# Half of a projection's contraction by Strassen's products, the other half with the attention heads

## The chip, the cores and the metric

The kernel runs on one core of a Trainium2 chip. The metric is the device time of one execution in microseconds (us), lower is better. Engines: TensorE (PE) multiplies matrices and has a weight load (PEld) beside it; VectorE (DVE), ScalarE (ACT) and GpSimd (POOL) work element by element; SyncE (SP) issues the transfers (DMA). Each engine takes its instructions in a fixed order.

## The reference

One layer of an encoder with two kinds of attention heads. In short (`rms` divides by the root mean square and multiplies by a gain):

```python
u = rms(h, norm_w) @ w_in                         # (tokens, 2048) @ (2048, 6656)
qa, ka, va, za, qb, kb, vb, zb = split(u)         # 8 heads A (2 groups of k, v), 8 heads B, 128 wide
qa, ka = rope(rms(qa, q_norm_a)), rope(rms(ka, k_norm_a))
ya = softmax(qa @ ka.T / sqrt(128)) @ va * silu(za)          # every token to every token
qb, kb = rms(qb, q_norm_b), rms(kb, k_norm_b)
yb = (softmax over a window of 8 x 16 tokens, with a bias, and 16 meta tokens)(qb, kb, vb) * silu(zb)
out = h + concat(ya, yb) @ w_out                  # (tokens, 2048) @ (2048, 2048)
```

It is done for two sequences, a prompt of 1024 tokens and a sample of 256, each with the same 16 meta tokens ahead: 16 + 256 + 1024 = 1296 different tokens. All is float32.

## The kernel before

A full float32 product is made of three passes: both factors are split into a high part and a rest (`split`: ScalarE copies the high part, VectorE subtracts), and TensorE adds high x high, high x rest and rest x high. Features stand on the partitions. A strip is 128 of the 6656 columns of `w_in` (52 strips), and its contraction is 16 tiles of 128.

The tokens come in two chunks: `chunk1` has the meta tokens, the sample and 384 prompt tokens (656 in all), `chunk2` the other 640. `strips` runs a strip: for each of the 16 contraction tiles, three matmuls for each of two blocks of tokens (256 or 272, and 384; lines L128 to L130). `get_x` loads a tile of x when a strip first wants it, splits it unnormalised, and sums its squares; the tokens' scale is only known after the last tile, and is multiplied in when a strip's sums leave PSUM (`rb`, `eb`).

`chunk1` does the sample's attention and keeps its tokens' q, k, v and z in DRAM. `chunk2` then has for each head A four blocks of 256 prompt queries (`attend`; 52 matmuls each), between them `FILL_A` strips of the last `NL` heads B, so that TensorE has other work while VectorE and ScalarE make the softmax; then the first heads B with their windows (`attend_strip`). The blocks of the last `NL` heads B, the late blocks, are put between the column strips of the output projection (`outproj`): its first sixteen strips take only the mixed heads 0 to 7 and keep their sums (`pd`); at strip `LSTR` the heads 8 to 15 (`yh`) are loaded, and sixteen more strips finish. A block of attention has one chain: scores, the maximum over the keys (VectorE, then a reduction over the partitions on POOL), the subtraction, the exponential on ScalarE, the sum (again reduced on POOL), its reciprocal (`put_y`), the result `yt`, split and written to `yd`.

A scheduler sets the order in which each engine meets these pieces, from the order of the code, priorities (weights come 300 steps early) and the pools' buffers.

Of the kernel before, what the change touches and what calls it, by code (L numbers as in the profile page):

```python
# [12 lines left out]
F32 = mybir.dt.float32  # L13
F32R = mybir.dt.float32r
AF = mybir.ActivationFunctionType
ALU = mybir.AluOpType
# [3 lines left out]

P = 128
DM = 2048
KT = 16
NMETA = 16
# [3 lines left out]
C1P = 384  # L28
T1 = NMETA + NS + C1P
T2 = NP - C1P  # L30
# [7 lines left out]
NL = 4  # L38
FILL_A = 2
FILL_B = 1  # L40
LSTR = 12
YORD = (0, 4, 1, 5, 2, 6, 3, 7)
WCH = 4
OBL = [(0, 512), (512, 512), (1024, 256)]
QA, KA, VA, ZA, QB_, KB, VB, ZB = 0, 8, 10, 12, 20, 28, 36, 44


class Kern:
# [8 lines left out]
    def rsqrt(self, ms, n):  # L57

        nc = self.nc
        l = self.ev.tile([P, n], F32, tag="ev", name="rs_l")  # L60
        nc.scalar.activation(l[:], ms, AF.Ln)  # L61
        r0 = self.ev.tile([P, n], F32, tag="ev", name="rs_r0")
        nc.scalar.activation(r0[:], l[:], AF.Exp, scale=-0.5)
        nc.scalar.activation(l[:], r0[:], AF.Square, scale=0.5 ** 0.5)
        nc.vector.tensor_tensor(out=l[:], in0=ms, in1=l[:], op=ALU.mult)
        nc.vector.scalar_tensor_tensor(out=r0[:], in0=l[:], scalar=1.5, in1=r0[:], op0=ALU.subtract, op1=ALU.mult)
        return r0

    def start_chunk(self, src, T):

        self.xsrc, self.T, self.xs = src, T, {}
        self.acc = self.xr.tile([P, T], F32, tag="xr", name="xacc")
        self.rb = self.one.tile([P, T], F32, tag="rb", name="rb")
        self.eb = self.one.tile([P, T], F32, tag="eb", name="eb")

    def get_x(self, kt):
        nc = self.nc
        if kt not in self.xs:
            T, acc = self.T, self.acc
            r = self.xr.tile([P, T], F32, tag="xr", name="xr")  # L80
            self.lastx = nc.sync.dma_start(r[:], self.xsrc[:, kt, :]).ins
            h = self.x.tile([P, T], F32R, tag="xh", name="xh")
            l = self.x.tile([P, T], F32R, tag="xl", name="xl")
            w = self.nw[:, kt:kt + 1]
            nc.scalar.activation(h[:], r[:], AF.Copy, scale=w)  # L85
            nc.vector.scalar_tensor_tensor(out=l[:], in0=r[:], scalar=w, in1=h[:].bitcast(F32), op0=ALU.mult, op1=ALU.subtract)  # L86
            if kt == 0:
                nc.scalar.activation(acc[:], r[:], AF.Square, scale=DM ** -0.5)
            else:
                nc.scalar.activation(r[:], r[:], AF.Square, scale=DM ** -0.5)  # L90
                nc.vector.tensor_tensor(out=acc[:], in0=acc[:], in1=r[:], op=ALU.add)
            self.xs[kt] = (h[:], l[:])
            if kt == KT - 1:
                with self.tc.issue_after(self.lastx):
                    for d, c in self.consts:
                        nc.sync.dma_start(d[:], c)
                if self.xsrc is self.io["x1"]:
                    nc.scalar.mul(self.nqkw[:], self.qkw[:], -1.0)
                nc.gpsimd.partition_all_reduce(self.eb[:], acc[:], P, RED.add)
                nc.vector.tensor_scalar(out=self.eb[:], in0=self.eb[:], scalar1=EPS, scalar2=None, op0=ALU.add)  # L100
                for o in range(0, T, 328):
                    n = min(328, T - o)
                    rr = self.rsqrt(self.eb[:, o:o + n], n)
                    nc.scalar.mul(self.rb[:, o:o + n], rr[:], -1.0)
                nc.vector.tensor_scalar(out=self.eb[:], in0=self.eb[:], scalar1=EPS, scalar2=None, op0=ALU.mult)
        return self.xs[kt]

    def strips(self, jobs, getx):

        nc, tc = self.nc, self.tc  # L110
        out = [[pool.tile([P, 512], F32, tag=tag, name="pp") for pool, tag in pools] for _, _, pools in jobs]
        for c in range(KT // WCH):
            ws = []
            for src, _, _ in jobs:
                with tc.high_priority(offset=self.woff):
                    w = self.raw.tile([P, WCH, P], F32, tag="raw", name="wr")
                    self.lastw = nc.sync.dma_start(w[:], src[:, c * WCH:(c + 1) * WCH, :]).ins
                    wh = self.w.tile([P, WCH, P], F32R, tag="wh", name="wh")
                    wl = self.w.tile([P, WCH, P], F32R, tag="wl", name="wl")
                    self.split(wh[:], wl[:], w[:])  # L120
                    ws.append((wh, wl))
            for k in range(WCH):
                kt = c * WCH + k
                xh, xl = getx(kt)
                for (wh, wl), ps, (_, blocks, _) in zip(ws, out, jobs):
                    for p, (o, n) in zip(ps, blocks):
                        first, last = kt == 0, kt == KT - 1
                        nc.tensor.matmul(p[:, :n], wh[:, k, :], xh[:, o:o + n], start=first, stop=False)  # L128
# [773 lines left out]
```

## Time and profile before

| | |
|---|---|
| median of three runs | 2295.93 us (2295.69 to 2296.95) |
| the profiled execution | 2295.91 us, span 2294.1 us |
| TensorE busy | 2268.6 us, 99% |
| VectorE busy | 1601.9 us, 70% |
| ScalarE busy | 1104.6 us, 48% |
| POOL busy | 530.9 us, 23% |
| DMA, mean | 126 GB/s, 39.5% of the engines' time |

The span runs from the first to the last instruction; the time has 1.8 us more. Busy time is what the recorded instructions take; where matmuls are pipelined, their starts tell more than their durations, since these overlap. An instruction's row ends with the idle time of its engine ahead of it and with what ended it, where there was any.

### The profile page before, as it was taken

Reading aid. Unit: us, or ns where it says so; the run is one execution under the profiler, and the core shown is the slowest. Engines: PE = TensorE matmul, PEld = TensorE weight load, DVE = VectorE, ACT = ScalarE, POOL = GpSimd, SP = SyncE. Lnnn points to the kernel's source line nnn. Section 1 sums busy time; section 2 is a strip of 40 time slices with the busy share of each in tenths; the row PEclk is TensorE's granted clock in tenths of the full one; section 3 lists DMA queues with packets and bytes.
Section 4 is the critical chain, followed back from the end, with each engine's and each line's share of the span. In section 5 each row is a group of like instructions: output and inputs, shape, how many; then the busy total and the mean of one; then the engine's idle time right before and its main releaser. Section 6 shows DMA issues by size and latency. Waiting matters only on the chain.

```text
span 2294.1 us, 40464 instructions
## 1 busy us (share of the span) xinstructions
PE 2268.6 (99%) x15166; PEld 2192.9 (96%) x15166; DVE 1601.9 (70%) x3092; ACT 1104.6 (48%) x2400; POOL 530.9 (23%) x275
## 2 busy tenths in 40 slices
PE   7999999999999999999999999999999999999999
PEld 7999999999999999999999999999999888888888
DVE  6876775555555689999998989998777666652221
ACT  6654554444444566676666665665454333320000
POOL 0322232211121124223223314223233222210000
PEclk9999999999999999999999999999999999999999
DMA  6433333333333442222222222224444966657342
GB/s 199 137 111 112 110 105 111 107 106 106 102 108 107 134 153 72 90 86 75 91 93 87 88 81 75 87 84 138 116 133 115 336 214 191 191 182 277 133 136 79
DMA packets 205733, 290.17 MB, mean 126 GB/s; under 512 B 55360, under 2 KB 125408, under 8 KB 203488
## 3 DMA queue, kind: packets, MB, share of 16 engines
q1 hardware_dynamic: 205536, 287.58, 39.5%
q8 instruction: 119, 1.95, 0.4%
q14 instruction: 78, 0.64, 0.1%
HBM read 216.30 MB, written 64.63 MB: 122 GB/s over the span
## 4 chain that ended last, share of the span: by engine, by line
PE 54%; DVE 3%; ACT 1%; POOL 1%; issue 1%; DMA 1%; SPq 0%; DVEq 0%; POOLq 0%
PE pp L130 8%; PE pp L129 8%; PE pp L128 8%; PE pp L754 7%; PE pp L755 7%; PE pp L756 7%; PE po L393 2%; PE po L296 1%; PE po L294 1%; PE po L295 1%; PE sp L254 1%; PE sp L255 1%; PE sp L256 1%; POOL m L138 1%; PE sp L361 1%
## 5 line engine op out<-in xcount | busy, mean ns | idle before, releaser
L128 PE MATMUL pp<-xh,wh 128*128 128x384 f32 (+2 forms) x3328 | 1025.2, 311 | 11.8 <-ACT xh L85 11.6
L129 PE MATMUL pp<-xl,wh 128*128 128x384 f32 (+2 forms) x3328 | 1030.7, 310 | 1.1 <-DVE xl L86 0.8
L130 PE MATMUL pp<-xh,wl 128*128 128x384 f32 (+2 forms) x3328 | 1029.8, 311 | 0.0
L128 PEld LDWEIGHTS pp<-xh,wh 128*128 128x128 f32 x3328 | 624.1, 188 | 13.7 <-ACT xh L85 13.1
L129 PEld LDWEIGHTS pp<-xl,wh 128*128 128x128 f32 x3328 | 625.8, 188 | 3.4 <-DVE xl L86 3.3
L130 PEld LDWEIGHTS pp<-xh,wl 128*128 128x128 f32 x3328 | 625.7, 188 | 0.2
L55 DVE TENSOR_TENSOR wl<-wr,wh 128x512 fp32r<-128x512 f32 x480 | 368.7, 771 | 226.1 <-ACT wh L54 220.8
L54 ACT CAST wh<-wr 128x512 fp32r<-128x512 f32 x480 | 294.7, 617 | 416.2 <-PE pp L129 198.3
L138 POOL PARTITION_ALL_REDUCE m<-ms x104 | 246.4, 2369 | 423.2 <-ACT ms L136 299.9
L754 PE MATMUL pp<-yh,wh 128*128 128x512 f32 (+1 forms) x768 | 274.6, 358 | 2.5 <-DMA yh<-yd 2.5
L755 PE MATMUL pp<-yh,wh 128*128 128x512 f32 (+1 forms) x768 | 275.0, 358 | 0.0
L219 POOL PARTITION_ALL_REDUCE tot<-a x80 | 170.3, 2128 | 450.6 <-DVE a L217 450.5
L756 PE MATMUL pp<-yh,wl 128*128 128x512 f32 (+1 forms) x768 | 274.2, 358 | 0.0
L202 POOL PARTITION_ALL_REDUCE ma<-m x80 | 106.9, 1336 | 583.9 <-DVE m L200 570.2
L754 PEld LDWEIGHTS pp<-yh,wh 128*128 128x128 f32 x768 | 145.7, 190 | 24.0 <-DMA yh<-yd 2.6
L755 PEld LDWEIGHTS pp<-yh,wh 128*128 128x128 f32 x768 | 145.7, 190 | 20.9
L756 PEld LDWEIGHTS pp<-yh,wl 128*128 128x128 f32 x768 | 145.5, 190 | 20.8
L785 DVE TENSOR_TENSOR o<-pp,o 128x512 f32<-128x512 f32 (+1 forms) x48 | 28.5, 602 | 140.3 <-PE pp L756 140.3
L258 ACT COPY S<-sp 128x512 f32<-128x512 f32 x136 | 77.7, 581 | 61.1 <-PE sp L256 37.1
L275 ACT ACTIVATE S<-S 128x512 f32<-128x512 f32 x136 | 84.4, 629 | 30.1 <-DVE S L274 30.0
L61 ACT ACTIVATE rs_l<-m 128x384 f32<-128x384 f32 (+2 forms) x104 | 49.1, 472 | 102.4 <-DVE m L139 102.2
L55 DVE TENSOR_TENSOR pl<-S,ph 128x512 fp32r<-128x512 f32 x136 | 96.0, 719 | 0.0
(186 smaller groups left out, 3235.6 us busy)
## 6 DMA issues: line engine op xcount, KB each, us to landing
wr<-in_w_in SPq DMA_DIRECT2D x416, 256.0 KB, 3.2
yd<-yt SPq DMA_DIRECT2D x160, 128.0 KB, 2.4
yh<-yd SPq DMA_DIRECT2D x16, 1280.0 KB, 17.4
wr<-in_w_out SPq DMA_DIRECT2D x64, 256.0 KB, 4.0
pd<-o SPq DMA_DIRECT2D x16, 640.0 KB, 4.3
o<-pd SPq DMA_DIRECT2D x16, 640.0 KB, 5.0
bt<-in_bt SPq DMA_DIRECT2D x16, 576.0 KB, 5.3
vw<-vn SPq DMA_DIRECT2D x32, 256.0 KB, 3.6
```

The lines of the kernel that those rows point to most:

```text
L54: nc.scalar.copy(hi, full)
L55: nc.vector.tensor_tensor(out=lo, in0=full, in1=hi.bitcast(F32), op=ALU.subtract)
L128: nc.tensor.matmul(p[:, :n], wh[:, k, :], xh[:, o:o + n], start=first, stop=False)
L129: nc.tensor.matmul(p[:, :n], wh[:, k, :], xl[:, o:o + n], start=False, stop=False)
L130: nc.tensor.matmul(p[:, :n], wl[:, k, :], xh[:, o:o + n], start=False, stop=last)
L138: nc.gpsimd.partition_all_reduce(m2[:], ms[:], P, RED.add)
L202: nc.gpsimd.partition_all_reduce(ma[:], m1[:], P, RED.max)
L219: nc.gpsimd.partition_all_reduce(tot[:], a1[:], P, RED.add)
L275: nc.scalar.activation(s, s, AF.Exp, scale=SCALE)
L754: nc.tensor.matmul(p[:, :n], wh, yh[:, o:o + n], start=i == 0, stop=False)
L755: nc.tensor.matmul(p[:, :n], wh, yl[:, o:o + n], start=False, stop=False)
L756: nc.tensor.matmul(p[:, :n], wl, yh[:, o:o + n], start=False, stop=i == 7)
```

## The change

The contraction of the first projection is cut in two. `first_half` takes the contraction tiles 0 to 7 for all 1296 tokens and all 52 strips. Two strips, two halves of the tokens and two quarters of the contraction make a 2 x 2 by 2 x 2 product, and `strassen` does it with seven products in place of eight (the variant with few sums); each product is four tiles x two blocks of 320 or 328 columns x three passes. `operands` loads all of x, normalises it and builds the seven sets of token operands once; `mixed` builds the weights' for each pair of strips. The 26 pairs' sums go to DRAM (`ud`). Between the pairs, `ahead` splits x's tiles 8 to 15 and the weights of 32 strips for later, and keeps them in DRAM (`xd`, `wd`).

`second_half` loads the split x, and runs every strip's remaining eight tiles for all tokens at once (`project`; blocks of 272 or 256, 512 and 512), adds the kept sum (`add_kept`) and goes on as before. With no chunks, a head has five blocks (`run`: four of the prompt and one of the sample). The late heads are six in place of four, with five blocks each, spread over the first 13 column strips of the output projection; `FILL_B` is gone.

```diff
-NL = 4
-FILL_A = 2
-FILL_B = 1
-LSTR = 12
+NL = 6
+FILL_A = 3
+LSTR = 13
...
+ORDER = (1, 2, 5, 6, 3, 7, 4)
...
+    def mm(self, ps, w, x, k, o, first, last):
+        for b in range(2):
+            p = ps[:, b, o:HB]
+            wh, wl = w[:, 0, k, :], w[:, 1, k, :]
+            xh, xl = x[:, 0, b, o:], x[:, 1, b, o:]
+            self.nc.tensor.matmul(p, wh, xh, start=first, stop=False)
+            self.nc.tensor.matmul(p, wh, xl, start=False, stop=False)
+            self.nc.tensor.matmul(p, wl, xh, start=False, stop=last)
+    def product(self, w, x, o):
+        ps = self.bank()
+        for k in range(WCH):
+            self.mm(ps, w, x[k], k, o, k == 0, k == WCH - 1)
+        return ps
...
+    def token_scale(self, half):
+        nc = self.nc
+        acc = self.rb[half]
+        (m, r), (l, _) = self.stage("b22", 2 * half), self.stage("b22", 2 * half + 1)
+        nc.gpsimd.partition_all_reduce(m, acc[:], P, RED.add)
+        self.rsqrt(m, r, l)
+        nc.scalar.mul(acc[:], r, -1.0)
...
+        raw = [[self.stage(n, k) for n in ("t2", "t3")] for k in range(WCH)]
+        for half in range(2):
+            for kt in range(KT):
+                r, sq = self.stage("t4", kt % WCH)
+                if kt < KH:
+                    r = raw[kt % WCH][half][kt // WCH]
+                nc.sync.dma_start(r, io[f"x{half + 1}"][:, kt].rearrange("p (b c) -> p b c", b=2))
+                acc = self.rb[half][:]
+                nc.scalar.activation(sq if kt else acc, r, AF.Square, scale=DM ** -0.5)
+                if kt:
+                    nc.vector.tensor_tensor(out=acc, in0=acc, in1=sq, op=ALU.add)
+            self.token_scale(half)
+        self.B = B = {n: [None] * WCH for n in self.bm}
...
+        for c, n in enumerate(("b11", "b21")):
+            for k in range(WCH):
+                put(n, k, norm(0, c, k))
+        for k in range(WCH):
+            t1 = raw[k][0][0]
+            minus(t1, norm(1, 0, k), t1)
+            put("t1", k, t1)
+        for k in range(WCH):
+            t2, t4 = self.stage("b22", k)
+            minus(t2, norm(1, 1, k), raw[k][0][0])
+            minus(t4, raw[k][0][1], t2)
+            put("t2", k, t2)
+            put("t4", k, t4)
+        for k in range(WCH):
+            b22 = raw[k][1][1]
+            put("b22", k, b22)
+            t3 = self.ct("t3")[:]
+            minus(t3, b22, raw[k][1][0])
+            put("t3", k, t3)
...
+        mix(s1, a21, a22, ALU.add)
+        mix(s2, s1, a11, ALU.subtract)
+        mix(a21, a11, a21, ALU.subtract)
+        mix(s4, a12, s2, ALU.subtract)
+        return {1: a11, 5: s1, 6: s2, 3: s4, 7: a21, 2: a12, 4: a22}
...
+        def p2():
+            ps, c = self.product(w[2], B["b21"], o), self.ct("c11")
+            add(c, ps, t["u"], o)
+            self.keep_sum(2 * i, 0, c)
+        def p3():
+            ps, c = self.product(w[3], B["b22"], HM), self.ct("c12")
+            add(c, t["u"], t["p5"], HM)
+            add(c, ps, c, HM)
+            self.keep_sum(2 * i, 1, c)
...
+    def first_half(self):
+        tc = self.tc
+        w = [{}, {}]
+        more = [self.ps.tile([P, 2, WCH, P], F32, tag="ps", name="wr") for _ in range(2)]
+        full = [self.mixed(0, [self.wraw(self.raw, "raw") for _ in range(4)]), self.mixed(1, [t[:, j] for t in more for j in range(2)])]
+        self.operands()
+        steps = [self.strassen(i, w[i]) for i in range(2)]
+        for n in ORDER:
+            for i in range(2):
+                w[i][n] = self.wsplit(full[i][n])
+                steps[i][n]()
+        ahead = self.ahead()
+        units = 4 * KH + 2 * len(AHEAD)
+        n, done = NW // 2 - 2, 0
+        for i in range(n):
+            with tc.high_priority(offset=self.woff):
+                full = self.mixed(2 + i, [self.wraw(self.raw, "raw") for _ in range(4)])
+                w = {k: self.wsplit(full[k]) for k in ORDER}
+            step = self.strassen(2 + i, w)
+            for k in ORDER:
+                step[k]()
+            while done * (n - 1) < units * (i + 1) and next(ahead, self) is not self:
+                done += 1
...
+    def tile_products(self, ps, ws, kt, o, n):
+        wh, wl = (ws[kt // WCH][:, i, kt % WCH, :] for i in range(2))
+        xh, xl = (self.xs[kt][:, i, o:o + n] for i in range(2))
+        first, last = kt == 0, kt == KH - 1
+        self.nc.tensor.matmul(ps[:, :n], wh, xh, start=first, stop=False)
+        self.nc.tensor.matmul(ps[:, :n], wh, xl, start=False, stop=False)
+        self.nc.tensor.matmul(ps[:, :n], wl, xh, start=False, stop=last)
+    def add_kept(self, ps, u, n):
+        self.nc.vector.tensor_tensor(out=u[:], in0=ps[:, :n], in1=u[:], op=ALU.add)
+        return u
+    def project(self, s, blocks, evac, result=None):
+        ws, us = self.weights(s), self.kept(s, blocks)
+        for j, ((o, n), u) in enumerate(zip(blocks, us)):
+            ps = self.pp.tile([P, 512], F32, tag="pp", name="pp")
+            for kt in range(KH):
+                self.tile_products(ps, ws, kt, o, n)
+            evac(j, self.add_kept(ps, u, n), o, n)
+        return result
...
+    def run(self, h, *a):
+        for b in range(5):
+            self.run_block(h, b, *a)
+    def late_blocks(self):
+        for h in range(NH - NL, NH):
+            k, v = self.k_load(h), self.v_windows(h)
+            tab, q, z = self.bias_table(h), self.q_load(h), self.z_load(h)
+            for b in range(5):
+                self.run_block(NH + h, b, q, z, k, v, tab)
+                yield
...
-        done = 0
+        late, blocks, done = self.late_blocks(), 5 * NL, 0
         for c in range(16):
-            while done < 4 * NL and done * LSTR < 4 * NL * (c + 1):
-                next(self.late_blocks)
+            while done < blocks and done * LSTR < blocks * (c + 1):
+                next(late)
                 done += 1
```

Three places in the engines' orders. The first is VectorE at the start; `xl` is the rest of a tile of x, `xacc` and `rb` the sum of squares, `stage` a raw or built tile, `b_493` the first split operand. Before:

```order
L55 TENSOR_TENSOR wl<-wr,wh 128x512
L86 SCALAR_TENSOR_TENSOR xl<-xr,nw,xh 128x656
L55 TENSOR_TENSOR wl<-wr,wh 128x512 x3
L86 SCALAR_TENSOR_TENSOR xl<-xr,nw,xh 128x656 x2
L91 TENSOR_TENSOR xacc<-xacc,xr 128x656
```

and now, behind five splits and six mixes of weights and the first sum:

```order
L158 TENSOR_TENSOR rb<-rb,stage 128x656 x24
L78 SCALAR_TENSOR_TENSOR stage<-stage 128x656
L158 TENSOR_TENSOR rb<-rb,stage 128x656
L79 SCALAR_TENSOR_TENSOR stage<-stage 128x656
L158 TENSOR_TENSOR rb<-rb,stage 128x656 x2
L164 SCALAR_TENSOR_TENSOR stage<-stage,nw,rb 128x656 x6
L158 TENSOR_TENSOR rb<-rb,stage 128x656
L164 SCALAR_TENSOR_TENSOR stage<-stage,nw,rb 128x656 x2
L66 TENSOR_TENSOR b_493<-stage,b_493 128x656
```

The first split of x was the second thing on VectorE, and now stands behind sums, scale and multiplications; L78 and L79 are the scale of the first half of the tokens.

The second is TensorE in the prompt's attention; `sp` are scores, `po` values, `pp` a strip's sums. Before:

```order
L254 MATMUL sp<-q,kf 128x256
L255 MATMUL sp<-q,kf 128x256
L256 MATMUL sp<-q,kf 128x256
L128 MATMUL pp<-xh,wh 128x256
L129 MATMUL pp<-xl,wh 128x256
L130 MATMUL pp<-xh,wl 128x256
L128 MATMUL pp<-xh,wh 128x384
L129 MATMUL pp<-xl,wh 128x384
L190 MATMUL sm_ps<-q,km 48x256
```

and now, the end of one of the runs (58 matmuls from the last `pp` to the next):

```order
L519 MATMUL po<-ph,va 128x256
L520 MATMUL po<-ph,va 128x256
L521 MATMUL po<-pl,va 128x256
L522 MATMUL po<-Pm,vm_7131 128x256
L479 MATMUL sp<-q,kf 128x256
L480 MATMUL sp<-q,kf 128x256
L481 MATMUL sp<-q,kf 128x256
```

Scores and values that had a strip's matmuls between them follow each other.

The third is VectorE under the late blocks at the end; L217 and now L442 are a block's sum, L228 and now L453 its reciprocal, L382 and now L607 the subtraction of the maximum, L779 the evacuation of the output projection (now L877). Before, from one block's sum to the next maximum:

```order
L217 TENSOR_TENSOR a_24464<-a_24464,Sm 16x256
L779 TENSOR_TENSOR o<-pp,o 128x512
L228 TENSOR_TENSOR tot<-tot,r 128x256
L779 TENSOR_TENSOR o<-pp,o 128x512
L229 SCALAR_TENSOR_TENSOR r<-tot,r 128x256
L232 TENSOR_TENSOR y<-po,z 128x256
L375 TENSOR_TENSOR m_24607<-S 128x256
L236 SCALAR_TENSOR_TENSOR y<-y,r 128x256
L378 TENSOR_TENSOR m_24607<-m_24607,S 128x128
L200 TENSOR_TENSOR m_24607<-m_24607,Sm 16x256
```

and now:

```order
L442 TENSOR_TENSOR a_21115<-a_21115,Sm 16x256
L591 SCALAR_TENSOR_TENSOR S<-sp,bt 128x256
L591 SCALAR_TENSOR_TENSOR S<-sp,bt 128x384
L457 TENSOR_TENSOR y<-po,z 128x256
L600 TENSOR_TENSOR m_21254<-S 128x256
L453 TENSOR_TENSOR tot<-tot,r 128x256
L603 TENSOR_TENSOR m_21254<-m_21254,S 128x128
L454 SCALAR_TENSOR_TENSOR r<-tot,r 128x256
L425 TENSOR_TENSOR m_21254<-m_21254,Sm 16x256
L461 SCALAR_TENSOR_TENSOR y<-y,r 128x256
L66 TENSOR_TENSOR yt<-y,yt 128x256
L607 TENSOR_TENSOR S<-S,ma 128x256
```

The evacuations and the weight splits that stood between the steps are gone from the last 13 blocks. On TensorE these blocks end in one piece:

```order
L417 MATMUL sp<-q,km 48x256
L615 MATMUL po<-Pm,vm_7131 128x256
L618 MATMUL po<-S,vw 128x128 x2
L618 MATMUL po<-S,vw 128x192 x2
L555 MATMUL po<-Pm,vm_7131 128x256
L558 MATMUL po<-S,vs 128x64 x4
L855 MATMUL pp<-yh,w 128x512
```

Before, values stood inside the output projection:

```order
L754 MATMUL pp<-yh,wh 128x256
L755 MATMUL pp<-yh,wh 128x256
L390 MATMUL po<-Pm,vm_255 128x256
L393 MATMUL po<-S,vw 128x128 x2
L393 MATMUL po<-S,vw 128x192 x2
L756 MATMUL pp<-yh,wl 128x256
```

The last matmuls of the late blocks had the output projection's on both sides, and now stand by themselves.

More of the change, by code (lines that the diff above doesn't have):

```diff
@@ L23 @@
 KT = 16
+KH = 8
 NMETA = 16
@@ L108, in strips @@
[L108 to L121, printed above, removed]
-            for k in range(WCH):
[L123 to L128, printed above, removed]
-                        nc.tensor.matmul(p[:, :n], wh[:, k, :], xl[:, o:o + n], start=False, stop=False)
-                        nc.tensor.matmul(p[:, :n], wl[:, k, :], xh[:, o:o + n], start=False, stop=last)
-        return out
```

707 lines of the change are left out of this document (344 added, 363 removed).

## Prediction

> **What bounds the kernel now.** I read the page's first parts, then the timeline of TensorE inside the projections, then a table of stretches.
>
> ```profile
> span 2294.1 us, 40464 instructions
> ...
> PE 2268.6 (99%) x15166; PEld 2192.9 (96%) x15166; DVE 1601.9 (70%) x3092; ACT 1104.6 (48%) x2400; POOL 530.9 (23%) x275
> ...
> PE   7999999999999999999999999999999999999999
> ```
>
> TensorE works nearly all the time; only the first of forty slices is below 9. So work taken from TensorE shortens the kernel, but only as long as the rest still covers every wait. The span is 2294.1 us, and the same execution's time 2295.91 us, 1.8 us more; the median of the three runs, 2295.93 us, is the same.
>
> ```profile
> 400.66 0.34 PE L128 MATMUL pp<-xh,wh 128*128 128x384 f32 x1
> ...
> 401.19 0.28 PE L128 MATMUL pp<-xh,wh 128*128 128x256 f32 x1
> ...
> 401.55 0.34 PE L128 MATMUL pp<-xh,wh 128*128 128x384 f32 x1
> ...
> 402.43 0.34 PE L128 MATMUL pp<-xh,wh 128*128 128x384 f32 x1
> ```
>
> Ends are modelled, so I cost matmuls from start to start. Three of 256 columns take 401.55 - 401.19 = 0.36 us, 120 ns each; two cycles of six take 402.43 - 400.66 = 1.77 us, which leaves (1.77 - 0.72) / 6 = 175 ns for 384. The slope is 0.43 ns a column: 127 ns at 272, 147.5 at 320, 151 at 328.
>
> ```profile
> 0.00:57.00 57.00, 45.28 (x275) 42.21 (x276) 37.26 (x48) 35.90 (x55) 5.67 (x10) 1.00 0.64 198
> 57.00:820.00 763.00, 762.71 (x5246) 762.10 (x5245) 481.13 (x890) 366.32 (x803) 167.20 (x84) 1.00 0.36 114
> 820.00:1550.00 730.00, 723.52 (x5227) 718.26 (x5226) 673.38 (x1263) 478.17 (x1036) 224.33 (x103) 1.00 0.28 88
> 1830.00:2070.00 240.00, 240.00 (x1393) 210.38 (x1392) 153.89 (x359) 75.38 (x174) 49.11 (x33) 1.00 0.64 199
> 2070.00:2294.00 224.00, 220.40 (x1152) 189.79 (x1150) 49.06 (x79) 17.91 (x30) 0.00 (x0) 1.00 0.43 150
> ```
>
> Columns: stretch, length, busy time of PE, weight loads, DVE, ACT and POOL, TensorE's clock, DMA share, GB/s. The last row holds the second half of the output projection, 768 matmuls of 512 columns and 384 of 256: 220.4 us / 1152 = 191 ns, so 512 columns take 227 ns. Waits exist only at the start (57.0 - 45.3 = 12 us). From 820 to 1550, the prompt attention with its filler strips, DVE is busy 92%: there two engines are nearly full. From 1830 to 2070 the late attention blocks run under the output projection, and TensorE loses nothing.
>
> **Matmuls.** Before, the projections have 4992 matmuls of 384 columns, 4032 of 256 and 960 of 272: 873.6 + 483.8 + 121.9 = 1479 us. After, the first half of the contraction has 7 products x 26 pairs x 24 = 4368, of which 3168 with 320 columns and 1200 with 328, and the second half 2496 of 512, 768 of 256 and 480 of 272: 467.3 + 181.2 + 566.6 + 92.2 + 61.0 = 1368 us. That is 111 us less; the 227 ns come from a stretch without other work, and five more nanoseconds on 2496 matmuls are 12 us, so I take **-105** (98 to 111). Attention and the output projection keep their matmuls. The Trainium skill ("TensorE: Matmul & The Clock Gate", Back-to-back issue gap) gives N/2.4 + 2.5 ns for a single warm matmul; by it the saving would be an estimated 87 us, but the trace's 227 ns at 512 columns stands above its 216, and 175 at 384 above its 162.
>
> **Start.** Before, TensorE starts with the first tile of x, unnormalised. Strassen adds operands of both token halves and both contraction quarters, so now all 32 tiles of x are loaded, squared and summed, reduced over the partitions, inverted, multiplied in, subtracted and split before the seven products can run.
>
> ```profile
> 1790.00:1820.00 30.00, 29.92 (x142) 25.36 (x143) 14.01 (x37) 7.07 (x17) 5.75 (x4) 0.90 0.96 371
> ...
> L99 POOL PARTITION_ALL_REDUCE eb<-xacc x2 | 8.4, 4193 | 49.6 <-DVE xacc L91 49.6
> ...
> L86 DVE SCALAR_TENSOR_TENSOR xl<-xr,nw,xh 128x656 fp32r<-128x656 f32 x16 | 14.3, 900 | 8.2 <-ACT xh L85 8.2
> ...
> L91 DVE TENSOR_TENSOR xacc<-xacc,xr 128x656 f32<-128x656 f32 x15 | 12.6, 838 | 2.3 <-ACT xr L90 1.9
> ```
>
> Transfers: 32 tiles of 0.33 MB and 2.1 MB of weights are 12.8 MB. The first 57 us moved 198 GB/s at a share of 0.64, so about 310 GB/s if full (371 at 0.96 in the other row): x1 is in at about 37 us with the weights, x2 near 54. VectorE stands in order, and its order puts 24 of the 30 sums, nine of them of x2, ahead of the first half's scale; I put that scale at 53 us (37, nine tiles of 1.06 us, the all-reduce of 4.2 beside them, a chain of about 5). Behind it VectorE has 16 multiplications (0.90), 16 subtractions (0.84) and 28 splits (0.84), 51 us, and some 14 us of sums of products: 53 + 51 + 14 = 118, and the last products bring the first two pairs to 127 us. Their work on TensorE is 14 x 3.55 = 50 us, so 77 stand idle, 65 more than the 12 before, less 3 for the slow first matmuls that before also had: **+62**. From below +45 (instructions start about 0.1 us before the one ahead ends), from above +75 (transfers at 198 GB/s).
>
> **Strassen itself.**
>
> ```profile
> L55 DVE TENSOR_TENSOR wl<-wr,wh 128x512 fp32r<-128x512 f32 x480 | 368.7, 771 | 226.1 <-ACT wh L54 220.8
> ```
>
> Per pair TensorE has 168 matmuls, 24.8 us; VectorE has 4 mixes and 7 splits of weights at 0.77 and 9 sums of 640 columns at about 0.84, 16 us, and a little of the second half's splits; ScalarE has less. DMA: sums to DRAM 34.5 MB, split weights 33.5, split x 10.6, reads 49, 128 MB in some 620 us or 206 GB/s, under the 371 above: hidden. At the seam, the second half's eight x tiles (1.3 MB each) go where operands were, about 24 us under the last pair. I put **+5** (0 to 15). Adding the kept sum is one more instruction for each evacuation on VectorE, but three blocks replace four, and the scale multiplications go: nothing, since VectorE has slack in this half.
>
> **Prompt attention.** Where projection matmuls stand between a block's scores and values, they cover VectorE. In TensorE's new order 18 runs of 24 to 70 attention matmuls, 686 together, have no projection between them; before there is none here.
>
> ```profile
> L55 DVE TENSOR_TENSOR pl<-S,ph 128x512 fp32r<-128x512 f32 x136 | 96.0, 719 | 0.0
> L274 DVE TENSOR_TENSOR S<-S,ma 128x512 f32<-128x512 f32 x136 | 88.5, 706 | 3.0 <-POOL ma L202 2.9
> ...
> L280 DVE TENSOR_TENSOR acc<-acc,S 128x512 f32<-128x512 f32 x64 | 45.7, 714 | 0.2
> L264 DVE TENSOR_TENSOR mx<-mx,sp 128x512 f32<-128x512 f32 x64 | 43.2, 675 | 3.8 <-ACT S L258 3.8
> ```
>
> A block is 52 matmuls of 256 columns, 6.2 us. On VectorE it is 4 x (0.71 + 0.65) + 3 x (0.71 + 0.68) = 9.6 us (busy over count) and about 3.5 of small instructions: 13 against 6.2. 686 matmuls are 13 blocks, so all exposed it is 13 x 6.9 = 90 us; nothing if five score buffers and other strips hide it. Most runs are shorter than one block, so I take 40%: **+36** (0 to 90).
>
> **Tail.** NL grows from 4 to 6 and the blocks of a head from 4 to 5: 30 late blocks in place of 16. In the new order TensorE has 215 attention matmuls in one piece, with no output projection among them, behind the last matmul of the first sixteen column strips, and VectorE has 13 block sums (L442) behind the last evacuation (L877): 12 intervals, 9 of strip blocks, 3 of sample blocks, each serial.
>
> ```profile
> 1848.36 0.41 DVE L217 TENSOR_TENSOR a<-a,Sm 16x256 f32<-16x256 f32 x1
> 1851.74 0.42 DVE L228 TENSOR_TENSOR tot<-tot,r 128x256 f32<-128x256 f32 x1 [2.96 <-ACT r L227]
> ...
> 1859.67 0.41 DVE L382 TENSOR_TENSOR S<-S,ma 128x256 f32<-128x256 f32 x1
> ...
> 1861.14 0.43 DVE L375 TENSOR_TENSOR a<-S 128x256 f32<-128x256 f32 x1 [0.27 <-ACT S L386]
> ...
> 1862.37 0.41 DVE L217 TENSOR_TENSOR a<-a,Sm 16x256 f32<-16x256 f32 x1
> ...
> L202 POOL PARTITION_ALL_REDUCE ma<-m x80 | 106.9, 1336 | 583.9 <-DVE m L200 570.2 <-ACT yt L54 5.4 <-DVE yt L55 4.3
> ...
> L217 DVE TENSOR_TENSOR a<-a,Sm x5: 412/413/414, 1994.2 to 2044.8; 16x256 f32<-16x256 f32 x5
> ...
> L730 SPq DMA_DIRECT2D yh<-yd x8: 390/468/585, 2053.8 to 2057.6; - x8
> ...
> DMA to landing us min/median/max: 7.0/15.9/25.5
> ```
>
> One interval: sum to reciprocal 1851.74 - 1848.36 = 3.4 us, two small instructions and the next block's maximum 0.9, POOL's maximum and the step to the subtraction 1.6, exponential 1861.14 - 1859.67 = 1.5, the sums 1862.37 - 1861.14 = 1.2: 8.6 us. A sample block I put at 7.3, and 4 us for the split of the next head's k and q: 9 x 8.6 + 3 x 7.3 + 4 = 103. Behind it the last y goes to DRAM (about 6 us) and comes back (7.0 at least, the load being queued on SP right behind the writes): 116 us. In it TensorE has about 31 us to do (215 x 0.14), so 85 idle, against some 5 before by the starts: **+80**. From below, VectorE's own work in an interval is about 5.9 us: 71 + 13 - 31 - 5 = +48; from above, before's spacing under full load, 50.6 / 4 = 12.65 us: 152 + 13 - 31 - 5 = +129.
>
> ```profile
> 1790.08 0.80 PE L754 MATMUL pp<-yh,wh 128*128 128x512 f32 x1 [2.46 <-DMA yh<-yd]
> ```
>
> At the start of the output projection TensorE waited 2.46 us for yh. Now these loads stand on SP behind weights' that wait until x's tiles come free: a load that starts late costs up to its 7.0 us, so **+5** (0 to 10).
>
> **Sum.** 2294.1 - 105 + 62 + 5 + 36 + 80 + 5 = 2377, and 1.8 outside the span: **2379 us**.
>
> **Rivals.**
> - The attention costs less than I say but the kernel is still slower: runs in the prompt part hidden, tail at 5.9 us. 2379 - 36 - 32 = 2311; somewhere from there to 2355.
> - Prompt attention is bound by VectorE's chain wherever no strip stands: 90 in place of 36, 2433. For it: 92% DVE before; against: VectorE has 717 us of work there by count, TensorE 840.
> - The tail runs at before's spacing: 129 in place of 80, 2428. Against: that spacing has evacuations and weight splits in it, the tail none.
> - The clock falls in the tail.
>
> ```profile
> 8.97 0.53 PE L129 MATMUL pp<-xl,wh 128*128 128x384 f32 x1
> 9.29 0.53 PE L130 MATMUL pp<-xh,wl 128*128 128x384 f32 x1
> 9.61 0.43 PE L128 MATMUL pp<-xh,wh 128*128 128x272 f32 x1
> ```
>
> At the start a 384-column matmul takes 0.32 us from start to start, nearly twice the 0.175, and after 2.46 us of idle at 1790 one of 512 took 0.80. If each interval's matmuls run so, TensorE's 31 us become 62, mostly beside VectorE's chain; values that VectorE waits for may add 1.5 us an interval: +18, 2397. The Trainium skill (same page, "HAM oscillation — how this bites in real kernels") puts the limit at idle gaps over about 3.4 us, which the tail's gaps would pass; the row at 1790 shows it after 2.46.
> - Faster: attention chains without projections in between are much shorter than the rows show, so that runs cost nothing and an interval falls to 4.2 us: the tail then adds 50 + 13 - 31 - 5 = 27, and 2294.1 - 105 + 62 + 5 + 27 + 5 + 1.8 = 2290. It is level with before at 4.7 us; VectorE's 5.9 us of instructions speaks against it.
> - That the change doesn't do what it says: TensorE's order holds 4368 + 3744 matmuls in place of 9984, so this is out.
>
> **Chances.** Forecast (2355 to 2405, bar the clock) 0.48; less attention, slower 0.16; prompt chain 0.10; slow tail 0.10; clock 0.07; faster 0.06; between, by some other mixture, 0.03. A measurement of this kernel can tell 0.2%, 4.6 us, from no change: slower 0.91, same 0.03, faster 0.06. The range leaves out the faster side, the lower part of the second case, and what the two upper cases give together: 2320 to 2440.
>
> **What would show it.** In the profile after: TensorE idle 70 to 85 us before about 127; nine-tenths busy or more in the rest of the first half, which then ends near 720; slices below 9 in the prompt attention; a stretch of some 116 us near the end with PE near a quarter, DVE sums about 8.6 us apart, and a clock below 1. Wrong would be: a tail whose intervals are below 5 us, a first pair done before 100 us, or a first half that waits for DMA or VectorE.

## The result and the profile after

The changed kernel takes 2693.0 us (median of four runs, 2689.95 to 2698.28) against 2295.81 us: 1.1733 times as long (95% interval 1.1713 to 1.1754), 397 us slower. The direction was forecast, the size was not: 2379 us, range 2320 to 2440. The profiled execution has a span of 2687.8 us.

First the parts of the page that were shown of before.

```profile
span 2687.8 us, 36415 instructions
...
PE 2294.1 (85%) x13294; PEld 2071.1 (77%) x13294; DVE 1755.0 (65%) x3096; ACT 1057.3 (39%) x2102; POOL 509.3 (19%) x250
...
PE   0698989899999999899678888885868999855999
...
PEclk9799999999999999999888899987888999956999
```

TensorE has 1872 instructions fewer and is busy no less: the row of its clock says why, since matmuls behind a wait run at a lower clock (0.56 in the tail's row below). Now the stretches, with the same columns as before.

```profile
0.00:134.00 134.00, 47.76 (x253) 45.81 (x254) 100.88 (x132) 61.23 (x91) 11.50 (x9) 0.90 0.35 119
134.00:540.00 406.00, 368.14 (x2420) 359.30 (x2420) 238.10 (x374) 120.43 (x218) 0.00 (x0) 1.00 0.73 240
540.00:793.00 253.00, 252.40 (x1698) 252.11 (x1698) 127.36 (x183) 55.31 (x91) 0.56 (x2) 1.00 0.36 119
...
860.00:1320.00 460.00, 431.74 (x2499) 375.75 (x2498) 408.09 (x713) 277.03 (x576) 167.31 (x71) 0.97 0.37 112
1320.00:1850.00 530.00, 417.94 (x2307) 364.67 (x2307) 423.47 (x723) 293.48 (x593) 166.49 (x73) 0.88 0.27 81
1850.00:2050.00 200.00, 144.23 (x719) 123.18 (x719) 113.84 (x211) 74.71 (x155) 47.82 (x23) 0.82 0.31 93
2340.00:2460.00 120.00, 58.38 (x260) 54.19 (x258) 79.50 (x206) 41.13 (x98) 37.61 (x25) 0.56 0.35 106
...
2460.00:2687.80 227.80, 223.60 (x1152) 192.18 (x1152) 47.00 (x75) 16.76 (x27) 0.00 (x0) 0.99 0.42 150
```

The table counts each stretch's matmuls at their undisturbed start-to-start times (231 ns for 512 columns, 151, 147, 124, 118 for 328, 320, 272, 256, 110 to 113 below) and takes the rest of its length as lost, to waits and to the slower clock behind them.

| stretch of the kernel after, us | lost | in that part before | more | forecast |
|---|---|---|---|---|
| start, 0 to 150 | 97 | 16 | +81 | +62 |
| Strassen and the seam, 150 to 860 | 55 | 2 | +53 | +5 |
| prompt attention, 860 to 1850 | 200 | 12 | +188 | +36 |
| heads B, start of the output projection, 1850 to 2050 | 78 | 10 | +68 | +5 |
| output projection with late blocks, 2050 to 2340 | 10 | 4 | +6 | |
| tail, 2340 to 2460 | 91 | 0 | +91 | +80 |
| rest | 5 | 2 | +3 | |
| all matmuls | 2153 | 2247 | -94 | -105 |

The sum of the rounded rows is +396 us; the spans differ by 394. Two stretches, 860 to 2050, hold 215 us that were not forecast. What TensorE waits for, in the whole kernel and then at one place (the waits' columns: us in total, times, longest; the timelines': start, duration):

```profile
PE pp L336 <- ACT w L65: 66.9, 17, 10.5
PE pa L108 <- ACT b L65: 60.4, 2, 58.0
PE sp L479 <- ACT q L65: 49.5, 6, 18.0
PE po L615 <- DVE Pm L437: 41.7, 9, 7.4
```

```profile
1339.04 0.80 PE L479 MATMUL sp<-q,kf 128*128 128x256 f32 x2 [18.02 <-ACT q L65]
...
1337.19 2.41 SPq L380 DMA_DIRECT2D ts<-t  x4
1339.69 1.03 SPq L124 DMA_DIRECT2D wr<-in_w_in  x2
...
1343.51 0.62 ACT L65 CAST w<-wr 128x512 fp32r<-128x512 f32 x1 [1.69 <-DMA wr<-in_w_in]
```

L336 is a strip's first matmul in the second half, L65 the cast that makes its weights' high part; L479 is the first score of a head, which needs the last block of q. Both appear where a strip's weights were not split ahead: before 1320 us `AHEAD` serves every strip, behind it 20 of them load raw weights (L124) themselves. At 1339 such a load is only issued behind the last rope transfer of q (`ts`), although its place in the program is 300 steps early. `weights` takes the raw tile from `ev`, the seven buffers that evacuations use.

### The profile page after: what moved, and what is told of

It reads as the page before. It is cut to its first block, busy times and chain, and to the rows that moved or that the text cites. A ratio compares the mean times of both kernels' runs of the same rounds, so it can differ in the third digit from the quotient of the medians.

```text
span 2687.8 us, 36415 instructions
## 1 busy us (share of the span) xinstructions
PE 2294.1 (85%) x13294; PEld 2071.1 (77%) x13294; DVE 1755.0 (65%) x3096; ACT 1057.3 (39%) x2102; POOL 509.3 (19%) x250
## 4 chain that ended last, share of the span: by engine, by line
PE 49%; DMA 19%; DVE 17%; ACT 6%; issue 4%; POOL 2%; SPq 2%; DVEq 0%; ACTq 0%; POOLq 0%
PE pp L336 5%; PE pp L855 5%; PE pp L856 5%; PE pp L857 5%; PE pp L337 5%; PE pp L338 5%; DMA ws<-in_w_in 4%; DMA wr<-in_w_in 4%; DMA wd<-ws 3%; PE pa L108 3%; PE pa L109 3%; PE pa L110 3%; DMA xs<-in_x 1%; PE po L618 1%; DVE l L78 1%
## 5 line engine op out<-in xcount | busy, mean ns | idle before, releaser
L336 PE MATMUL pp<-x,w 128*128 128x512 f32 (+2 forms) x1248 | 463.2, 372 | 79.8 <-ACT w L65 66.9
L337 PE MATMUL pp<-x,w 128*128 128x512 f32 (+2 forms) x1248 | 459.6, 369 | 0.0
L338 PE MATMUL pp<-x,w 128*128 128x512 f32 (+2 forms) x1248 | 449.3, 365 | 0.0
L65 ACT CAST w<-wr 128x512 fp32r<-128x512 f32 x286 | 172.2, 618 | 434.2 <-PE pp L857 203.3
L336 PEld LDWEIGHTS pp<-x,w 128*128 128x128 f32 x1248 | 246.7, 198 | 119.9 <-ACT w L65 71.6
L108 PE MATMUL pa<-t,w 128*128 128x320 f32 (+1 forms) x832 | 263.0, 317 | 40.2 <-DVE u L219 14.7
L375 POOL PARTITION_ALL_REDUCE ms<-l x78 | 228.1, 2925 | 316.0 <-ACT l L374 262.3
L855 PE MATMUL pp<-yh,w 128*128 128x512 f32 (+1 forms) x768 | 275.9, 359 | 14.0 <-DMA yh<-yd 14.0
L856 PE MATMUL pp<-yh,w 128*128 128x512 f32 (+1 forms) x768 | 275.3, 359 | 0.0
L857 PE MATMUL pp<-yh,w 128*128 128x512 f32 (+1 forms) x768 | 274.5, 358 | 0.0
L337 PEld LDWEIGHTS pp<-x,w 128*128 128x128 f32 x1248 | 246.4, 198 | 32.7
L66 DVE TENSOR_TENSOR w<-wr,w 128x512 fp32r<-128x512 f32 x286 | 194.9, 688 | 114.2 <-ACT w L65 113.8
L338 PEld LDWEIGHTS pp<-x,w 128*128 128x128 f32 x1248 | 241.4, 194 | 32.8
L108 PE MATMUL pa<-b,w 128*128 128x320 f32 (+1 forms) x624 | 199.1, 320 | 77.9 <-ACT b L65 60.4
L109 PE MATMUL pa<-t,w 128*128 128x320 f32 (+1 forms) x832 | 259.5, 312 | 4.3 <-DVE t L66 4.3
L110 PE MATMUL pa<-t,w 128*128 128x320 f32 (+1 forms) x832 | 259.2, 312 | 0.0
L444 POOL PARTITION_ALL_REDUCE tot<-a x80 | 169.4, 2117 | 420.2 <-DVE a L442 420.2
L109 PE MATMUL pa<-b,w 128*128 128x320 f32 (+1 forms) x624 | 196.1, 314 | 2.3 <-DVE b L66 2.3
L110 PE MATMUL pa<-b,w 128*128 128x320 f32 (+1 forms) x624 | 195.3, 313 | 0.0
L108 PEld LDWEIGHTS pa<-t,w 128*128 128x128 f32 x832 | 158.1, 190 | 46.2 <-ACT w L65 12.7
L108 PEld LDWEIGHTS pa<-b,w 128*128 128x128 f32 x624 | 119.8, 192 | 82.2 <-ACT b L65 60.8
```

Source lines behind the costliest of these rows:

```text
L65: nc.scalar.copy(hi, full)
L66: nc.vector.tensor_tensor(out=lo, in0=full, in1=hi.bitcast(F32), op=ALU.subtract)
L108: self.nc.tensor.matmul(p, wh, xh, start=first, stop=False)
L109: self.nc.tensor.matmul(p, wh, xl, start=False, stop=False)
L110: self.nc.tensor.matmul(p, wl, xh, start=False, stop=last)
L336: self.nc.tensor.matmul(ps[:, :n], wh, xh, start=first, stop=False)
```

## The experiments

Each run is one execution beside one of the kernel before (2293 to 2298 us); the four of the changed kernel lie within 8.4 us. A run differs by its diff from the changed kernel, or from the run or kernel that its text names. "Lost" is counted as in the table.

**All weights ahead.**

```diff
-for _h in range(NH - NL, NH - NL + 3):
+for _h in (2, 3, 4, 5, 6, 7, 0, 1):
     AHEAD += [KB + _h, QB_ + _h, VB + _h, ZB + _h]
```

> The weights of all 52 strips, not of 32, are split in the first half and kept in DRAM; nothing else is changed. Late-weights theory: from 1320 us on, where the strips that are not split ahead begin, raw weights are loaded into evacuation buffers by a queue that stands behind the rope transfers, and TensorE waits 66.9 us for ScalarE's weight casts and then runs at a lower clock; the time falls from 2693 by 80 to 130 us, the stretch from 1320 to 2060 from 740 us to some 640, and the row of the weight casts goes from the waits. VectorE theory (TensorE's cover in the second half is simply too small for VectorE and the attention chains): the waits move to other releasers, the time falls by less than 30 us. The first half may become up to 30 us longer by 31 MB more of transfers.

2551.8 us, 141 less, a little above the range. The weight casts leave TensorE's list of waits, and q's wait goes with them, from 49.5 to 11.5 us, though nothing in q's evacuation was changed. The first half ends at 820 in place of 793. So late weights hold, and hold up q as well; the VectorE theory falls for this part.

**q before z.**

```diff
-                z = pr(*self.z_strip(ZA + h))
                 q = pr(*self.q_strip(QA + h, qw, True))
+                z = pr(*self.z_strip(ZA + h))
```

> For the heads A the q strip comes before the z strip. Exposed-chain theory: the attention of a head begins with its scores, which need the last block of q, and q's evacuation is about 9 us a block, three blocks in series; z's 72 matmuls (13.6 us) then cover it: TensorE's wait of 49.5 us for q's casts falls below 15, the time by 40 to 70 us. VectorE theory: the waits move, less than 20 us.

2674.8 us, 18 less, where the exposed chain promised 40 to 70. q's wait is off the list's head, but the wait for weights grew from 66.9 to 83.3 us: the exposed chain looks like a second sign of the same shortage.

**Nine evacuation buffers.**

```diff
-                pools(es_w, ("w", 5))
+                pools(es_w, ("w", 4))
...
-                pools(es_proj, ("pu", 4), ("ev", 7))
+                pools(es_proj, ("pu", 4), ("ev", 9))
```

> Nine evacuation buffers in place of seven (a q block takes five), paid for with one weight buffer of the w pool (four in place of five). Buffer theory: seven buffers let only one q or k block be evacuated at a time, and hold raw weights as well; with nine two blocks overlap in part: waits for q's casts fall from 49.5 to about 25, those for weights from 66.9 to about 40, 40 to 70 us less in all. Against: one weight buffer less may cost 10 to 40 us in the first half. VectorE theory: no gain, the time between 2680 and 2720.

2649.8 us, 43 less, but not as expected: 18 us come from the first half, which ends at 775 with four w buffers (why fewer serve it better was not tried), and the waits only go from 66.9 to 58.0 and from 49.5 to 44.7. More buffers of the shared kind hardly help.

**Four late heads.**

```diff
-NL = 6
-FILL_A = 3
+NL = 4
+FILL_A = 2
```

> Four late heads as before the change, in place of six, and two filler strips a head, in place of three: 20 late blocks under the output projection, 12 of the 16 late strips split ahead. Tail theory: the piece of 91 us idle near 2340 to 2460 falls below 20, since 20 blocks of 12 to 13 us fit into the 307 us of the first sixteen column strips. What the four heads B in the middle then cost shows what the tail was traded for: by the VectorE theory they wait about as much as the tail did (time within 2660 to 2720), by the late-weights theory the strips ahead serve more of the prompt part, and the time falls by 60 to 120 us.

2696.3 us, the same. The tail is gone (24 us lost in the whole stretch from 2154 to 2460), and the middle has it:

```profile
1716.00:2154.00 438.00, 326.29 (x1638) 279.57 (x1637) 277.07 (x520) 179.22 (x378) 132.21 (x62) 0.82 0.29 87
```

This is the heads B between prompt attention and output projection; 161 of 438 us are lost there. By its range this speaks for the VectorE theory; but the weights come late there too (45 us of TensorE's waits in this stretch are for their casts), so it does not tell the two theories apart.

**Buffers of their own for raw weights.** AHEAD stays at 32 strips.

```diff
-                pools(es_w, ("w", 5))
+                pools(es_w, ("w", 4))
...
-                    w = self.wsplit(self.wload(self.wraw(self.ev, "ev"), s, 2 + c))
+                    w = self.wsplit(self.wload(self.wraw(self.rw, "rw"), s, 2 + c))
...
-                pools(es_proj, ("pu", 4), ("ev", 7))
+                pools(es_proj, ("pu", 4), ("ev", 7), ("rw", 2))
```

> As the changed kernel (32 strips' weights ahead), but the raw weights of the other 20 strips have two buffers of their own and take none of the seven evacuation buffers; paid for with one of five w buffers, as in the run with nine evacuation buffers. Buffer theory: raw weights came late because they waited for evacuation buffers, and q's evacuation waited for those that they held; both waits (66.9 and 49.5 us) fall below 30 together, the time to 2540 to 2590. Queue theory: the loads are issued late because they stand on the SP queue behind rope transfers that wait for ScalarE and VectorE, whatever buffers there are: L336's wait for casts stays above 40 us, the time between 2630 and 2660.

2520.5 us: 172 less than the changed kernel and 129 less than the run with nine buffers, which also has four w buffers and as many buffers of this size in all; the time is 20 below the range. TensorE's waits from 777 to 1882:

```profile
PE sp L479 <- ACT q L65: 11.8, 5, 3.4
PE pp L336 <- DVE u L341: 11.5, 5, 4.3
PE sp L480 <- DVE q L66: 10.3, 5, 2.7
```

The weights' casts are not among them. The prompt part now loses 98 us in place of 200, the heads B 21 in place of 78. So it is the sharing of the buffers; the queue theory, by which the loads are late whatever buffers there are, is out.

SP's order still has a part in it. The scheduler goes by the pools' buffers, and with the pool SP's order has changed as well. In the changed kernel the first loads of raw weights, at 1339.69, stand behind 21 rounds of rope transfers (four `ts` each), and so they do with nine shared buffers; with buffers of their own they stand ahead of all of these, and the next two behind 18:

```profile
783.89 3.46 SPq L124 DMA_DIRECT2D wr<-in_w_in  x2
...
1291.67 4.28 SPq L124 DMA_DIRECT2D wr<-in_w_in  x2
```

Whether a shared tile came late for want of a free buffer, or for the place in SP's order that the shared pool gave its load, no run here separates.

**No strip's weights ahead, buffers shared.**

```diff
-for _h in range(NH - NL, NH - NL + 3):
-    AHEAD += [KB + _h, QB_ + _h, VB + _h, ZB + _h]
+AHEAD = []
```

> No strip's weights are split ahead, only x's second half; all 52 strips load raw weights into evacuation buffers in the second half. Late-weights theory: the loss of some 7 us a strip that 20 strips showed (141 us) now falls on 52: the second half up to the output projection becomes 120 to 220 us longer than the changed kernel's 1258 us. The first half tells what the ahead work costs it: if its 38 us of waits between 134 and 540 come from VectorE standing behind ahead splits that wait for DMA, it ends 30 to 45 us earlier than 793; if they come from Strassen's own sums, within 10 us of 793.

2928.7 us. The second half up to the output projection takes 1515 us in place of 1258 (776 to 2291), 257 more, above the range. Lines are one lower in this kernel:

```profile
PE pp L335 <- ACT w L64: 189.8, 43, 15.2
PE sp L478 <- ACT q L64: 76.3, 8, 9.8
```

The first half ends at 760, 33 us earlier: with five w buffers that is what VectorE's and the queues' work for later strips costs Strassen. About 18 us stay lost without it. The first strip of the second half then waits 15.2 us for its weights, until 776.

**Both, and then five late heads.** The first has all weights ahead, nine evacuation and four w buffers; the second also `NL = 5`.

> All 52 strips' weights ahead, and nine evacuation buffers with four w buffers. If late weights and short buffers are separate costs, 2552 - 43 = 2509; if the buffers only mattered because raw weights held some of them, the gain is that of the first half alone (18 us): 2530 to 2540.

> As the run before it, with five late heads in place of six: 25 late blocks, so five or six of the tail's 12 intervals of 8.8 us go, and a third head B with its five blocks comes into the middle part. Tail theory: the tail's idle time falls from 91 to 95 us to 40 to 50, and the middle part gives back 10 to 30: 15 to 40 us less than the run before it. If the middle part is bound by VectorE, it gives all of it back.

2522.3 and 2522.1 us. The first lies between its two alternatives. Its first half ends at 794, where that of all weights ahead alone ends at 820, and this is 26 of the 29 us gained. So the reason of the second holds, with more than its 18 us: the buffers mattered because raw weights held some of them. All ahead and short of nothing, it equals the run with buffers of their own (2520.5). In the second the tail loses 67 us in place of 96, and the heads B 50 in place of 19: all given back, as the VectorE theory said for the middle.

**No strip's weights ahead, raw buffers of their own.** As the run with the raw pool, with `AHEAD = []`.

> Raw weights in buffers of their own, as in the run with that pool (2520.5 us), and no strip's weights ahead: 52 strips load raw weights in the second half. Buffer theory: where 52 strips cost 257 us more than 32 ahead when they shared the evacuation buffers, they now cost little: the first half ends 20 to 35 us earlier than 777, the second half gains 44 us of VectorE's splits (64 of 0.69), of which the prompt part, with VectorE at 90%, shows 15 to 40: 2490 to 2530. Queue theory, that late loads come from SP's order: some 7 us a strip remain, above 2650.

2556.8 us, above the range. The first half does end 20 us earlier (757), but the first strip of the second half then waits 18.3 us for its weights, and the prompt part loses 145 us in place of 98, as VectorE and ScalarE split 82 raw tiles there in place of 31. The step from 32 ahead to none, which cost 236 us with shared buffers, costs 36.

**Less VectorE.** The run with the raw pool, with two VectorE and one ScalarE instruction fewer for each reciprocal root; it leaves out the roots' Newton step.

```diff
-        nc.scalar.activation(l, out, AF.Square, scale=0.5 ** 0.5)
-        nc.vector.scalar_tensor_tensor(out=l, in0=m, scalar=EPS, in1=l, op0=ALU.add, op1=ALU.mult)
-        nc.vector.scalar_tensor_tensor(out=out, in0=l, scalar=1.5, in1=out, op0=ALU.subtract, op1=ALU.mult)
```

> The run with the raw pool, without the Newton step (a sign goes with it) in the reciprocal roots of the norms: for each evacuated block of q and k one ScalarE and two VectorE instructions less, 48.6 + 41.3 = 90 us of VectorE between 860 and 1750. VectorE theory for what is left of the prompt part (98 us over the ideal, VectorE busy 89 and 92%): it gets 50 to 90 us shorter, 2430 to 2470 in all. Order theory (runs of attention without strips between, whose chains pass POOL and ScalarE): below 25 us, above 2495.

2478.4 us, 42 less, between the two theories' ranges. The prompt part loses 62 us in place of 98. VectorE's load is a good part of what is left there, not all.

**No reduction on POOL.** The run with the raw pool; it leaves out the sum over the partitions in q's and k's norms.

```diff
-        nc.scalar.activation(l[:], u[:], AF.Square, scale=P ** -0.5)
-        nc.gpsimd.partition_all_reduce(ms[:], l[:], P, RED.add)
+        nc.scalar.activation(ms[:], u[:], AF.Square, scale=P ** -0.5)
```

> The run with the raw pool, without the reduction over the partitions of the squares in q's and k's evacuation (78 of 2.9 us on POOL; the squares themselves are used). VectorE's instructions that run beside these reductions take 64 us longer, together, than their like between 860 and 1750, mostly some of 1 to 3 us in place of 0.4 to 0.7. If POOL's reduction holds VectorE up, this excess falls from 76 to about 12 and the time by 40 to 80 us, to 2440 to 2480; if the excess has another cause, it stays, and only the chain of a q block gets 2.9 us shorter: 2500 to 2520.

2454.6 us, 66 less, inside the range; the excess, what VectorE's instructions take beyond their like, is 13 us. The subtraction of the maximum is 131 times the same instruction in both (first the run with the raw pool, then this one; ns as least, median, most):

```profile
L499 DVE TENSOR_TENSOR S<-S,ma x131: 669/682/2736, 879.7 to 1733.1; 128x512 f32<-128x512 f32 x131
```

```profile
L498 DVE TENSOR_TENSOR S<-S,ma x131: 673/685/694, 872.6 to 1671.5; 128x512 f32<-128x512 f32 x131
```

The prompt part loses 40 us. The chain of a q block also got shorter by the reduction itself; the two were not taken apart.

**The kernel before with shared buffers.**

```diff
-                    w = self.raw.tile([P, WCH, P], F32, tag="raw", name="wr")
+                    w = self.ev.tile([P, WCH, P], F32, tag="ev", name="wr")
...
-                tc.tile_pool(name="raw", bufs=4) as self.raw, tc.tile_pool(name="w", bufs=4) as self.w:
+                tc.tile_pool(name="raw", bufs=2) as self.raw, tc.tile_pool(name="w", bufs=4) as self.w:
```

> The kernel before, with the projection's raw weights in the nine evacuation buffers in place of four of their own (the output projection keeps two of its own). Buffer theory in its strong form, that sharing alone costs about 7 us a strip wherever evacuations and weights meet: 104 strip runs, 64 of them beside heavy evacuation, so 200 to 450 us more up to the output projection, which begins at 1790 before. Weak form, that sharing costs only where TensorE has little other work to bridge late weights: before, a strip's 96 matmuls in two chunks bridge most, and it costs below 60 us: 2295 to 2355.

3321.2 us, 1026 more, over twice the strong form's upper end. The output projection begins at 2819 in place of 1790 and takes 500 us in place of 504, so all of it lies ahead of that:

```profile
PE pp L128 <- ACT wh L54: 364.0, 79, 13.5
PE po L294 <- ACT ph L54: 82.7, 20, 8.5
PE sp L254 <- ACT qs L54: 63.7, 8, 8.0
```

Strips that bridge more did not help; the sharing alone is enough to cost a kernel 1026 us.

No version tried beats the kernel before. The best of those that leave no work out has the raw pool, at 2520.5 us.

## Why the prediction was wrong, step by step

**Matmuls: right in count, the saving a little short.** 4368 + 3744 as counted. In Strassen the 15 steps from the start at 700.22 to that at 702.43 are 147 ns each (147.5 forecast), 512 columns take 231 in the second half (227, with five more allowed). -94 against -105, and -98 was the end of the range.

**Start: right in its course, 19 us short.**

```profile
56.30 4.97 DVE L164 SCALAR_TENSOR_TENSOR stage<-stage,nw,rb 128x656 f32<-128x656 f32 x6 [0.61 <-ACT rb L100]
...
81.45 6.59 DVE L164 SCALAR_TENSOR_TENSOR stage<-stage,nw,rb 128x656 f32<-128x656 f32 x8 [0.82 <-ACT rb L100]
...
121.34 1.55 DVE L219 TENSOR_TENSOR c<-pa,u 128x640 f32<-128x640 f32 x2
...
122.31 0.60 PE L108 MATMUL pa<-b,w 128*128 128x320 f32 x1 [9.10 <-DVE c L219]
```

The first half's scale was put at 53 us and came at 56; the last operand was split at 120 (118). But six of the first fourteen products were still to run then, 21 us. The sum counted VectorE's 14 us of sums of products ahead of the last splits; their order puts them behind (the first sum that reads products, L219, at 121.34). These sums free PSUM, so TensorE stood 9.1 us for them and went on at 122.31 with a slow start; the first two pairs ended at 146, not 127.

**Strassen: the step that hid the ahead work was wrong.** +53 against +5. It was held to be below TensorE by its amounts (16 of 24.8 us on VectorE, 206 GB/s). From 134 to 540 it stood in front of it by its order: the sums that free PSUM wait on VectorE behind splits that wait for transfers. The waits of TensorE, VectorE and ScalarE in this stretch show the chain (`ws` are the weights for later):

```profile
PE pa L108 <- DVE u L219: 17.9, 15, 2.9
...
DVE ws L66 <- ACT ws L65: 88.8, 47, 5.0
...
ACT ws L65 <- DMA ws<-in_w_in: 177.1, 57, 5.6
```

Without the weights' part the first half ends 33 us sooner, and 20 sooner where there are four w buffers, which by themselves gave 18.

**Prompt attention and heads B: the step that failed.** +256 against +41, and the term behind it was not in the sum at all. The working costed the second half's strips by their matmuls and evacuations and never asked from which pool 20 strips take their raw weights. The runs show: 159 of these 256 us go with buffers of their own (188 - 86 and 68 - 11), and the time falls by 129 us against the same number of buffers in one shared pool. What remains, 86 us in the prompt part, fits the mechanism that was forecast, runs without strips and VectorE at 89 to 92%, about at its upper end of 90; 36 was too low, as 40% of 90 had no row behind it. Less VectorE work takes 36 us of it, no reduction on POOL 58: part of it is VectorE held up by POOL, which nothing in the working had. The wait for `yh` at the start of the output projection was 4.59 us, as put (5). The rival that bounded it by VectorE gave 2433; it was the nearest and still named the smaller part.

**Tail: right.**

```profile
L442 DVE TENSOR_TENSOR a<-a,Sm x13: 404/413/417, 2341.9 to 2448.3; 16x256 f32<-16x256 f32 x13
...
2341.94 0.41 DVE L442 TENSOR_TENSOR a<-a,Sm 16x256 f32<-16x256 f32 x1
2350.59 0.41 DVE L442 TENSOR_TENSOR a<-a,Sm 16x256 f32<-16x256 f32 x1
2357.92 0.41 DVE L442 TENSOR_TENSOR a<-a,Sm 16x256 f32<-16x256 f32 x1
```

12 intervals in 106.4 us (103), a strip block 8.7 (8.6), a sample block 7.3 (7.3), 91 us lost (85). In every kernel with six late heads it is 91 to 97.

**The clock: a rival for the tail, and a companion everywhere.** In the tail it is 0.56, and the intervals are no longer for it, so its +18 did not come. Elsewhere each wait was paid partly twice: from 1320 to 1850 TensorE is busy 417.9 us with matmuls that count 376, at a clock of 0.88. In the tail's bursts

```profile
2350.70 0.55 PE L615 MATMUL po<-Pm,vm 128*128 128x256 f32 x1 [5.66 <-DVE Pm L437]
...
2353.30 0.41 PE L585 MATMUL sp<-q,kf 128*128 128x128 f32 x1
...
2353.92 0.27 PE L585 MATMUL sp<-q,kf 128*128 128x128 f32 x1
```

the same matmul falls from 0.41 to 0.27 us about 3.2 us after the burst began. The Trainium skill ("TensorE: Matmul & The Clock Gate", "What's actually happening") has about 3.4 us of work until the full clock; the trace agrees.

Of the 314 us between forecast and result, the raw pool's run takes back 172, some 16 of them in the first half with its four w buffers. The other 141 are the terms' sizes: with weights out of the way, 16 from the start (78 lost more than before), 43 from Strassen and the seam, 50 from the prompt part, 6 from the heads B, 13 from the tail, 11 from the matmuls.

## What to carry to other kernels

When a change moves a load, follow where its buffer comes from before costing what the loaded data does: a tile fetched early out of a pool that later work also uses is fetched late, and holds that work up as well. Halving the matmuls of a stage halves the cover for all that stood beside them, so list, stage by stage, the waits that they hid, and price each; a gain in TensorE's count is only the first term. Work put "ahead" into a stage with slack on average still stands in its engines' orders, in front of what frees that stage's buffers.

## What the hardware showed that was not expected

A partition reduction on POOL holds up a VectorE instruction that runs beside it. In the run with the raw pool, VectorE and then POOL:

```profile
1354.76 3.94 DVE L499 TENSOR_TENSOR S<-S,ma 128x512 f32<-128x512 f32 x3
...
1354.68 3.26 POOL L375 PARTITION_ALL_REDUCE ms<-l  x1
```

Three subtractions that take 1.9 us elsewhere took 3.94, the first of them 2.73. From 860 to 1750 some 66 instructions take 76 us longer than their like, 64 us of it beside the reductions of q and k; with those reductions out 13 us are left. Not every instruction is held up: at 1110.92, inside a reduction of 2.17 us that began at 1109.28 (L444), a split (L66) takes its usual 0.68. The kernel before has it too, 46 us from 820 to 1550. The Trainium skill ("VectorE: DVE Perf Modes", "Two Vector instructions with no wait between them") says in passing that the second of two inputs in SBUF is read through an interface shared with GpSimd; that this is the cause fits, but no run here separates it from other causes.
